# Decode-state stores of a streaming encoder step: seven stores on the ScalarE queue become four on the SyncE queue, gathered in contiguous tiles

## The chip, the cores and the metric

The kernel runs on one core of one Trainium2 chip, as a single program. The metric is device time in microseconds. The engines are called PE (TensorE, matmul), PEld (its weight loads), DVE (VectorE), ACT (ScalarE), POOL (GpSimd) and SP (SyncE). SP computes nothing here: it issues DMAs. ACT issues DMAs too, between its own instructions. "ACTq" and "SPq" in a row are those issuing queues. L1127 is line 1127 of the kernel before.

## What is computed

One layer for two groups of requests: a prompt of 4096 rows, and a decode group of 8 streams of 16 rows. A normalised, modulated input is projected to nine parts; three branches (pooling, short convolution, spatial gating) are gated, projected back and added to the input. The pooling and convolution branches keep a history, and the new history is an output:

```python
def pool_mix(p, hist, pos0, w_pool, pool_scale):
    full = jnp.concatenate([hist, p], axis=1)
    ...
    return out, full[:, -POOL_HIST:]      # last 15 rows of 256 channels

def conv_mix(q, hist, w_conv):
    full = jnp.concatenate([hist, q], axis=1)
    out = sum(w_conv[k] * full[:, k:k + L] for k in range(CONV_K))
    return out, full[:, -CONV_HIST:]      # last 2 rows of 384 channels

def layer(...):
    ...
    y_pool, new_pool = pool_mix(p, pool_hist, pos0, w_pool, pool_scale)
    y_conv, new_conv = conv_mix(gc * hx, conv_hist, w_conv)
    vn = layernorm(v, v_norm_g, v_norm_b)
    ...
    return x + gate[:, None] * y, new_pool, new_conv, vn
```

For the decode group the outputs are `nps` (new pooling history, 8 streams of 15 rows), `ncs` (new convolution history, 8 streams of 2 rows) and `nvs` (the rows of vn); `npp` and `ncp` are the prompt's histories.

## The kernel before

The prompt is worked in eight blocks of 512 rows, the decode group as a ninth of 128 (8 streams of 16). Channels lie on the 128 partitions, rows along the free dimension. Float32 values are split in a high and a low half-precision part, and each product is three half-precision matmuls. Each block goes through an input stage (`in_block`, or `in_dec` for the decode group) and an output stage (`out_block`); the output stage of a block is issued after the input stage of the next one. So `in_dec` stands between the output stage of prompt block 6 and that of prompt block 7 (the `ox`, `oy`, `oz` matmuls of L1246), and the decode group's own output stage (L1287) ends the program.

**Weights** come from DRAM through a ring of 18 slots of 256 KB (tile `ws`, L224, on SP's queue), up to 16 slots ahead of use, in the order in which PE uses them. In `in_dec` these are eight pieces `w_v_parts`, four `w_pool_in_parts` and forty `w_in_parts`.

**in_dec** (L1097) multiplies v (`z_v`, L819), then the two pooling tiles (`pool_in`, `z_p`), then three convolution tiles (`conv(j)`), the two pooling outputs (`pool_out`) and three gating tiles. Each `plain()` is a product of 60 small matmuls on four weight slots (24 on two slots with `only1`), all of them `z` in the rows. `conv(j)` calls it twice. Its steps:

- ACT copies the first product out of PSUM (`gc`, L1122); POOL copies two history rows per stream in front (`q`, L1127; `q` has two buffers, so the third waits till the first is free); DVE writes the 16 new rows behind (L1128); ACT stores the last two rows of each stream to `ncs` (L1129).
- ACT and DVE apply the three taps (`c`, L748 and L750), DVE and ACT empty the second pair of products (L1132, and `sz`, L1134), and the result goes to `ya` (L739), whose size ACT measures (L743).

`pool_in(i)` writes 16 rows per stream behind 15 of history in `pe_s` (L1151) and the prompt's tail to `ph` (L1152), and ACT stores 15 rows per stream to `nps` (L1153). POOL makes the window sums (L774), DVE the differences `d` (L777). `pes` was filled by two loads from `stp` (L1451), one per channel half. `gmlp_v` normalises v; in the decode case DVE also makes `vn` (L855, L856), which ACT stores to `nvs` (L857). At the end of `in_dec` ACT stores `ph` to `npp` (L1181).

**The order on each queue** is made by the tile scheduler: it simulates the program, then writes one fixed instruction list for each engine, so the place of an instruction in the source isn't its place in the list. Each engine runs its list in order; a DMA stands in the list of the engine that issues it, and its waits hold up all that follows there. The framework gives every DMA of SP and ACT one of eight completion counters, `DMAHW0` to `DMAHW7`, in turn, whichever queue it is on; a DMA is issued only when the last one on its counter has landed.

In the stretch in question ACT also stores four result tiles of prompt block 6 (`out_y`, L1231, 512 KB each), which DVE finishes at L1230.

Of the kernel before, what the change touches and what calls it, by code (L numbers as in the profile page):

```python
# [10 lines left out]
F32 = mybir.dt.float32  # L11
# [7 lines left out]
P = 128  # L19
# [4 lines left out]
NB = 8  # L24
ND = 16
# [6 lines left out]
HIST = 15  # L32
# [44 lines left out]
def trunk_kernel(ctx, tc, x, xs, xT, xsT, cT, wada, bada, badag, ng, win, winpT, wout, wpool, pscale, wconv,  # L77
# [746 lines left out]
    def gmlp_v(b, vh, ts, given):  # L824

        c = inv_of["v", 0]
        if "cv2" not in state:
            state["cv2"] = con.tile([P, 1], F32, name="cv2")
            nc.vector.tensor_tensor(state["cv2"], c, c, ALU.mult)
        tt = len(ts)  # L830
        st = sm.tile([P, 2, 6], F32, tag="bst", name="bst", bufs=2)
        mv = sm.tile([P, 2, 2], F32, tag="bmv", name="bmv", bufs=2)
        pss = []
        for j, t in enumerate(ts):
            ps = given[j]
            nc.vector.bn_stats(st[:, j, :], ps)
            nc.vector.bn_aggr(mv[:, j, :], st[:, j, :])
            pss.append(ps)
        var = sm.tile([P, tt], F32, tag="var", name="var", bufs=2)
        nc.vector.tensor_scalar(var, mv[:, :tt, 1], state["cv2"], EPS, ALU.mult, ALU.add)  # L840
        r = rsqrt(var, tt)
        a = sm.tile([P, tt], F32, tag="va", name="va", bufs=2)
        nb = sm.tile([P, tt], F32, tag="vb", name="vb", bufs=2)
        nc.vector.tensor_scalar(a, r, c, 2.0 ** 10, ALU.mult, ALU.mult)
        nc.vector.scalar_tensor_tensor(nb, mv[:, :tt, 0], -1.0, a, ALU.mult, ALU.mult)
        for j, t in enumerate(ts):
            v = tp.tile([P, 384], F32, tag="v32", name="v32", bufs=2)
            nc.vector.tensor_scalar(v, pss[j], a[:, j:j + 1], nb[:, j:j + 1], ALU.mult, ALU.add)
            v3 = seg(v, 64)
            nc.scalar.copy(vh[:, 0, :, t, :], v3)  # L850
            nc.vector.tensor_tensor(vh[:, 1, :, t, :], v3, vh[:, 0, :, t, :], ALU.subtract)
            if b.dec:
                gb = state["gbl"]
                vn = tp.tile([P, 384], F32, tag="v32", name="vn", bufs=2)
                nc.vector.scalar_tensor_tensor(vn, v, 2.0 ** -10, gb[:, 0, :], ALU.mult, ALU.mult)  # L855
                nc.vector.tensor_tensor(vn, vn, gb[:, 1, :], ALU.add)  # L856
                nc.scalar.dma_start(nvs, vn)  # L857

    def gmlp_mix(b, i, vh):

# [236 lines left out]
    def in_dec(b, H):  # L1097
# [20 lines left out]
        def conv(j):  # L1118
            gcp, hxp = plain(2 * j)
            f = lambda g: inv_of[g, j]  # L1120
            gc = temp("gc", n)
            nc.scalar.activation(gc, gcp, AF.Identity, scale=f("gc"))  # L1122
            q = tp.tile([P, BT + 2], F32, tag="q", name="q", bufs=2)
            q = q[:, :NB * (ND + 2)].rearrange("p (s f) -> p s f", f=ND + 2)
            c = temp("c", n)
            at = lambda i: q[:, :, i:i + ND]
            nc.gpsimd.tensor_copy(q[:, :, 0:2], G["stc"][:, j])  # L1127
            nc.vector.scalar_tensor_tensor(at(2), seg(hxp), f("hx"), seg(gc), ALU.mult, ALU.mult)  # L1128
            nc.scalar.dma_start(ncs[:, j], q[:, :, ND:])  # L1129
            conv_taps(j, q, seg(c), at)  # L1130
            gbp, zcp = plain(2 * j + 1)
            nc.vector.scalar_tensor_tensor(c, gbp, f("gb"), c, ALU.mult, ALU.mult)  # L1132
            s = temp("sz", n)
            nc.scalar.activation(s, zcp, AF.Silu, scale=f("zc"))  # L1134
            finish(b, 2 + j, c, s, ya, ym)

        def pool_in(i):
            inv = state["pinv"]
            ps = psum("z_p")[:, :n + ND]
            for kh in range(2):  # L1140
                product(ps, as_parts(stream.get()), h(kh, n + ND), kh == 0, kh == 1)
            stream.ahead(4)
            wi = inv[:, i:i + 1]

            def ext(name):
                t = tp.tile([P, BT + 16], F32, tag="pw", name=name, bufs=4)
                return t[:, :NB * 32].rearrange("p (s f) -> p s f", f=32)

            cut = lambda t, a, z=None: t[:, :, a:z]
            pe, d = state["pes"][:, i], temp("d", n)  # L1150
            nc.scalar.activation(pe[:, :, 16:], seg(ps[:, :n]), AF.Identity, scale=wi)  # L1151
            nc.scalar.activation(G["ph"][:, i, :], ps[:, n + 1:], AF.Identity, scale=wi)  # L1152
            nc.scalar.dma_start(nps[:, i], pe[:, :, 17:])  # L1153
            for _ in windows(i, pe, seg(d), cut, ext):
                pass
            return d
# [17 lines left out]
        for i in range(3):  # L1174
# [3 lines left out]
            s = temp("sz", n)  # L1178
            nc.scalar.activation(s, zp, AF.Silu, scale=inv_of["zg", i])
            finish(b, 5 + i, m, s, ya, ym)  # L1180
        nc.scalar.dma_start(npp, G["ph"])  # L1181
        return ya, ym


# [247 lines left out]
    for b in blocks:  # L1432
        if b.dec:
            ya, ym = in_dec(b, H)
        elif b.i > 0:
            ya, ym = in_block(b, H)
        stream.ahead()
        if not b.dec:
            nb = blocks[b.i + 1]
            if nb.dec:  # L1440
                H = hprep_dec(nb, load_stats(nb))
                state["G"]["mixer"] = mixer(state["G"], True)
                mixer_bias(state["G"])
                last = hop.tile([P, 2, D], F32, tag="t", name="xg_s")
                nc.sync.dma_start(last[:, 0, :], xs)
                nc.sync.dma_start(last[:, 1, :], gsd)
                state["last"] = last
                pes = hop.tile([P, 2, NB, 2 * ND], F32, tag="S2", name="pe_s")
                gbl = hop.tile([P, 2, 384], F32, tag="S1", name="gb_ln")
                for i in range(2):  # L1450
                    nc.sync.dma_start(pes[:, i, :, 1:16], stp[:, i])  # L1451
                    nc.sync.dma_start(gbl[:, i, :], (lngr, lnbr)[i].broadcast_to([P, 384]))
                state["pes"], state["gbl"] = pes, gbl
            else:
                H = h_tiles()
                h_plain(H, state["t"])
                h_sums(H, state["t"])
        got = {}

        def mid(b=b, ya=ya, ym=ym, got=got):  # L1460
            got["iy"], got["sy"] = scale_y(ym)
            if b.dec:
                got["yh"] = split_y(b, ya, got["sy"])

        def done(b=b, ya=ya, got=got):
            if not b.dec:
                got["yh"] = split_y_fast(ya, got["sy"]) if b.i >= OUT_FAST else split_y(b, ya, got["sy"])
            return b, got["yh"], got["iy"]

        if b.i == 0:  # L1470
            state["first"] = lambda mid=mid, done=done: (mid(), state.update(prev=done()))
        else:
            out_block(*state["prev"], mid)
            state["prev"] = done()
# [92 lines left out]
```

## Time and profile before

| | us |
|---|---|
| time, median of 3 runs | 1446.16 |
| lowest and highest of the 3 | 1443.79, 1448.75 |
| the profiled execution's own time | 1448.44 |
| its span, first to last instruction | 1446.40 |
| PE busy | 1375.5 (95% of the span) |
| DVE busy | 998.8 (69%) |
| ACT busy | 639.6 (44%) |
| POOL busy | 112.4 (8%) |
| PE granted clock, mean | 0.987 |

How to read it: the span is that of one profiled execution; its own time has 2.04 us around the span. A row of a timeline gives start, duration, engine, line, operation, output tile and inputs, count, and in brackets how long the engine had stood idle before and what it then waited for. "issue" is waiting for which the profile shows no cause. In a row on DMAs, "us to landing" runs from the issue to the arrival of the last byte. PEclk is the granted clock as a share of full speed; the DMA share is the mean busy share of the core's 16 DMA engines (sums of packet times, so it can pass 1).

### The profile page before, as it was taken

Reading aid. Unit: us, or ns where it says so; the run is one execution under the profiler, and the core shown is the slowest. Engines: PE = TensorE matmul, PEld = TensorE weight load, DVE = VectorE, ACT = ScalarE, POOL = GpSimd, SP = SyncE. Lnnn points to the kernel's source line nnn. Section 1 sums busy time; section 2 is a strip of 40 time slices with the busy share of each in tenths; the row PEclk is TensorE's granted clock in tenths of the full one; section 3 lists DMA queues with packets and bytes.
Section 4 is the critical chain, followed back from the end, with each engine's and each line's share of the span. In section 5 each row is a group of like instructions: output and inputs, shape, how many; then the busy total and the mean of one; then the engine's idle time right before and its main releaser. Section 6 shows DMA issues by size and latency. Waiting matters only on the chain.

```text
span 1446.4 us, 27018 instructions
## 1 busy us (share of the span) xinstructions
PE 1375.5 (95%) x10228; PEld 963.8 (67%) x10228; DVE 998.8 (69%) x2109; ACT 639.6 (44%) x1232; POOL 112.4 (8%) x150
## 2 busy tenths in 40 slices
PE   5898999999999999999999999999999999999697
PEld 2443454684688747885688758884788568866563
DVE  4764798787896678777775668567955777356535
ACT  3765756653356344443453435544443344223111
POOL 0000200020020102000020002000100002001000
PEclk9999999999999999999999999999999999999889
DMA  9687955994769659787797769888776768778995
GB/s 361 225 301 254 344 162 208 371 368 137 261 205 346 217 164 343 252 296 257 246 323 257 203 221 353 280 281 314 274 261 199 210 214 274 201 227 240 224 286 167
DMA packets 188292, 373.30 MB, mean 258 GB/s; under 512 B 28801, under 2 KB 40833, under 8 KB 188161
## 3 DMA queue, kind: packets, MB, share of 16 engines
q1 hardware_dynamic: 176480, 351.92, 73.6%
q10 hardware_dynamic: 11680, 19.65, 3.8%
q8 instruction: 80, 1.31, 0.4%
q14 instruction: 52, 0.42, 0.1%
HBM read 311.10 MB, written 60.39 MB: 257 GB/s over the span
## 4 chain that ended last, share of the span: by engine, by line
PE 55%; DVE 14%; DMA 9%; ACT 3%; issue 2%; POOL 0%; SPq 0%; ACTq 0%; DVEq 0%
PE zx L676 17%; PE ox L1246 9%; PE zy L676 8%; PE ps_o L1313 5%; PE zz L676 4%; PE oy L1246 4%; PE z_v L819 2%; PE oz L1246 2%; DVE xr L1230 2%; DVE yh L161 1%; DMA xt<-in_x 1%; DMA ws<-w_in_parts 1%; DMA w_out_sums<-wt 1%; DVE d L777 1%; PE z L676 1%
## 5 line engine op out<-in xcount | busy, mean ns | idle before, releaser
L676 PEld LDWEIGHTS <-ws 128*128 128x128 f16 x6360 | 600.2, 99 | 120.9 <-issue 23.8
L676 PE MATMUL zx<-A,ws 128*128 128x256 f16 x1572 | 182.6, 273 | 2.3 <-DVE nzg L708 1.0
L676 PE MATMUL zy<-S,ws 128*128 128x256 f16 x1572 | 184.4, 273 | 0.1
L676 PE MATMUL zx<-S,ws 128*128 128x256 f16 x1440 | 169.6, 273 | 10.2 <-ACT nu L700 8.1
L1246 PEld LDWEIGHTS <-yh 128*128 128x128 f16 x1008 | 98.1, 98 | 116.1
L676 PEld LDWEIGHTS <-wp 128*128 128x128 f16 x1056 | 103.4, 99 | 74.6 <-issue 5.8
L1246 PE MATMUL ox<-ws,yh 128*128 128x512 f16 x576 | 128.6, 379 | 0.0
L676 PE MATMUL zq<-A,wp 128*128 128x512 f16 x528 | 115.6, 379 | 0.0
L819 PE MATMUL z_v<-ws,A 128*128 128x384 f16 x696 | 115.1, 326 | 0.0
L676 PE MATMUL zz<-A,ws 128*128 128x256 f16 x852 | 101.3, 273 | 0.0
L819 PEld LDWEIGHTS <-A 128*128 128x128 f16 x696 | 68.1, 98 | 46.3 <-DVE A L330 0.2
L160 ACT ACTIVATE yh<-ya,sy 128x1024 f16<-128x1024 f32 (+1 forms) x58 | 57.6, 1025 | 65.0 <-PE ox L1246 17.0
L1313 PE MATMUL ps_o<-ws,yh 128*128 128x512 f16 x384 | 83.6, 379 | 0.0
L161 DVE SCALAR_TENSOR_TENSOR yh<-ya,sy,yh 128x1024 f16<-128x1024 f32 (+1 forms) x58 | 64.6, 1137 | 7.7 <-ACT yh L160 7.6
L1225 ACT ACTIVATE junk<-xr 128x1024 bf16<-128x1024 f32 x32 | 33.4, 1045 | 80.5 <-DVE xr L1254 50.0
L1313 PEld LDWEIGHTS <-yh 128*128 128x128 f16 x384 | 37.4, 98 | 44.2
L1254 DVE SCALAR_TENSOR_TENSOR xr<-ox,io,xr 128x512 f32<-128x512 f32 x48 | 34.0, 745 | 46.8 <-PE ox L1246 43.7
L1246 PE MATMUL oy<-ws,yh 128*128 128x512 f16 x288 | 64.3, 379 | 0.0
L676 PE MATMUL zq<-A,ws 128*128 128x512 f16 x288 | 62.5, 379 | 0.0
L760 POOL COPY qh<-q 128x2 f32<-128x2 f32 x24 | 7.6, 318 | 588.8 <-DVE q L759 588.8
L750 DVE SCALAR_TENSOR_TENSOR c<-q,wconv_sb,c 128x512 f32<-128x512 f32 (+1 forms) x54 | 38.0, 704 | 17.4 <-ACT c L748 16.6
L676 PE MATMUL z<-A,ws 128*128 128x128 f16 x588 | 39.8, 235 | 9.1 <-ACT sz L1134 5.8
(289 smaller groups left out, 1911.2 us busy)
## 6 DMA issues: line engine op xcount, KB each, us to landing
ws<-w_in_parts SPq DMA_DIRECT2D x517, 256.0 KB, 4.5
ws<-w_out_parts SPq DMA_DIRECT2D x104, 256.0 KB, 4.8
ws<-w_out_sums SPq DMA_DIRECT2D x96, 256.0 KB, 4.2
w_in_parts<-wp SPq DMA_DIRECT2D x83, 256.0 KB, 4.8
t<-in_xT SPq DMA_DIRECT2D x32, 512.0 KB, 6.9
xr<-in_x SPq DMA_DIRECT2D x32, 512.0 KB, 6.4
out_y<-xr ACTq DMA_DIRECT2D x32, 512.0 KB, 5.8
xt<-in_x SPq DMA_DIRECT2D x28, 512.0 KB, 6.6
```

Of the source, the lines that this page charges most:

```text
L160: nc.scalar.activation(dst_hi, src, AF.Identity, scale=s)
L161: nc.vector.scalar_tensor_tensor(dst_lo, src, s, dst_hi, ALU.mult, ALU.subtract)
L676: nc.tensor.matmul(ps, w[:, a, k, :], h[:, c, k, :], start=first and i == 0, stop=last and i == 3 * KH - 1, skip_group_check=True)
L750: nc.vector.scalar_tensor_tensor(c, at(i), wc[:, j, i:i + 1], c, ALU.mult, ALU.add)
L760: nc.gpsimd.tensor_copy(G["qh"][:, j, :], q[:, n:n + 2])
L777: nc.vector.scalar_tensor_tensor(dv[rows], cut(sums[e], 16)[rows], state["G"]["cinv"][rows, i:i + 1], cut(pe, 16)[rows], ALU.mult, ALU.sub ...
L819: nc.tensor.matmul(pss[t], H[1 + k // KH][:, a, k % KH, t * P:(t + 1) * P], w[:, e, :], start=k == 0 and i == 0, stop=k == KT - 1 and i == 2)
L1225: nc.scalar.activation(junk.bitcast(BF16), xts[t], AF.Square, accum_out=ss[:, j:j + 1])
L1230: nc.vector.scalar_tensor_tensor(xts[t], xts[t], r[:, j:j + 1], state["O"]["fg"], ALU.mult, ALU.mult)
L1246: nc.tensor.matmul(pss[bank][t], op[p][:, a, k, t * P:(t + 1) * P], w[:, c, 0, :], start=first and k == 0 and i == 0, stop=k == KH - 1 and ...
L1254: nc.vector.scalar_tensor_tensor(xt, pss[bank][t], io[:, hf:hf + 1], xt, ALU.mult, ALU.add)
L1313: nc.tensor.matmul(pss[t], yh[:, a, k, t * P:(t + 1) * P], w[:, c, 0, :], start=k == 0 and i == 0, stop=k == KT - 1 and i == 2)
```

## The change

The last 15 pooling rows of each stream are no longer stored from `pe` by two DMAs; POOL copies them into one tile (`stp_s`), and the last two convolution rows into the tile that held the old ones (`stc_sb`). Each tile is stored by one DMA, written at the end of `in_dec`, on SP's queue. `npp` and `nvs` move to SP's queue too. The pooling history is loaded into `stp_s` by one DMA, and POOL copies it into `pes`.

```diff
--- before.py
+++ after.py
@@ -854,7 +854,7 @@
                 vn = tp.tile([P, 384], F32, tag="v32", name="vn", bufs=2)
                 nc.vector.scalar_tensor_tensor(vn, v, 2.0 ** -10, gb[:, 0, :], ALU.mult, ALU.mult)
                 nc.vector.tensor_tensor(vn, vn, gb[:, 1, :], ALU.add)
-                nc.scalar.dma_start(nvs, vn)
+                nc.sync.dma_start(nvs, vn)
 
     def gmlp_mix(b, i, vh):
 
@@ -1126,7 +1126,7 @@
             at = lambda i: q[:, :, i:i + ND]
             nc.gpsimd.tensor_copy(q[:, :, 0:2], G["stc"][:, j])
             nc.vector.scalar_tensor_tensor(at(2), seg(hxp), f("hx"), seg(gc), ALU.mult, ALU.mult)
-            nc.scalar.dma_start(ncs[:, j], q[:, :, ND:])
+            nc.gpsimd.tensor_copy(G["stc"][:, j], q[:, :, ND:])
             conv_taps(j, q, seg(c), at)
             gbp, zcp = plain(2 * j + 1)
             nc.vector.scalar_tensor_tensor(c, gbp, f("gb"), c, ALU.mult, ALU.mult)
@@ -1150,7 +1150,7 @@
             pe, d = state["pes"][:, i], temp("d", n)
             nc.scalar.activation(pe[:, :, 16:], seg(ps[:, :n]), AF.Identity, scale=wi)
             nc.scalar.activation(G["ph"][:, i, :], ps[:, n + 1:], AF.Identity, scale=wi)
-            nc.scalar.dma_start(nps[:, i], pe[:, :, 17:])
+            nc.gpsimd.tensor_copy(state["stp"][:, i], pe[:, :, 17:])
             for _ in windows(i, pe, seg(d), cut, ext):
                 pass
             return d
@@ -1178,7 +1178,9 @@
             s = temp("sz", n)
             nc.scalar.activation(s, zp, AF.Silu, scale=inv_of["zg", i])
             finish(b, 5 + i, m, s, ya, ym)
-        nc.scalar.dma_start(npp, G["ph"])
+        nc.sync.dma_start(npp, G["ph"])
+        nc.sync.dma_start(nps, state["stp"])
+        nc.sync.dma_start(ncs, G["stc"])
         return ya, ym
 
 
@@ -1447,8 +1449,11 @@
                 state["last"] = last
                 pes = hop.tile([P, 2, NB, 2 * ND], F32, tag="S2", name="pe_s")
                 gbl = hop.tile([P, 2, 384], F32, tag="S1", name="gb_ln")
+                states = hop.tile([P, 2, NB, HIST], F32, tag="A2s", name="stp_s")
+                state["stp"] = states
+                nc.sync.dma_start(states, stp)
                 for i in range(2):
-                    nc.sync.dma_start(pes[:, i, :, 1:16], stp[:, i])
+                    nc.gpsimd.tensor_copy(pes[:, i, :, 1:16], states[:, i])
                     nc.sync.dma_start(gbl[:, i, :], (lngr, lnbr)[i].broadcast_to([P, 384]))
                 state["pes"], state["gbl"] = pes, gbl
             else:
```

What the scheduler makes of it is seen in the lists. PE's list is the same but for one instruction pair (`ps_sum`, L152, of the decode group), which moves from among the first `oy` matmuls of block 7 to behind its second row of `ox`; DVE's changes order in a few places round it.

ACT, in `in_dec`, from the second `out_nps` to the taps of conv 1. Before:

```order
L1153 DMA out_nps<-pe_s 128x8x15 [waits DMAHW3_49,Activation_49]
L160 ACTIVATE yh<-ya,sy 128x1024 [waits DVE_49]
L1181 DMA out_npp<-ph 128x30 [waits DMAHW5_49,Activation_49]
L1122 ACTIVATE gc<-z_16289,w_i 128x128 [waits PE_49]
L160 ACTIVATE yh<-ya,sy 128x1024 [waits DVE_49]
L1129 DMA out_ncs<-q 128x8x2 [waits DMAHW4_49,DVE_49]
L748 ACTIVATE c<-q,wconv_sb 128x128
L1134 ACTIVATE sz<-z_16382,w_i 128x128 [waits PE_49]
L1122 ACTIVATE gc<-z_16444,w_i 128x128 [waits PE_49]
L743 ACTIVATE sz,ym<-ya 128x128 [waits DVE_49]
L1129 DMA out_ncs<-q 128x8x2 [waits DMAHW1_49,DVE_49]
L748 ACTIVATE c<-q,wconv_sb 128x128
```

The same place in the change:

```order
L160 ACTIVATE yh<-ya,sy 128x1024 [waits DVE_49]
L1122 ACTIVATE gc<-z_16291,w_i 128x128 [waits PE_49]
L160 ACTIVATE yh<-ya,sy 128x1024 [waits DVE_49]
L748 ACTIVATE c<-q,wconv_sb 128x128 [waits DVE_49]
L1134 ACTIVATE sz<-z_16384,w_i 128x128 [waits PE_49]
L1122 ACTIVATE gc<-z_16446,w_i 128x128 [waits PE_49]
L743 ACTIVATE sz,ym<-ya 128x128 [waits DVE_49]
L748 ACTIVATE c<-q,wconv_sb 128x128 [waits DVE_49]
L1233 DMA out_y<-xr 128x1024 [waits DMAHW0_49,DVE_49]
L1134 ACTIVATE sz<-z_16539,w_i 128x128 [waits PE_49]
```

The stores and their waits for a counter have left ACT's list; `out_y` (now L1233) stays, on other counters.

SP, where the weights of the decode part are loaded, in the change (before, the same list without the rows of `out_npp`, `out_nps` and `out_ncs`):

```order
L1181 DMA out_npp<-ph 128x30 [waits DMAHW0_49,Activation_49]
L224 DMA ws<-w_in_parts 128x1024 [waits DMAHW1_49,PE_49]
L224 DMA ws<-w_in_parts 128x1024 [waits DMAHW2_49,PE_49]
L1182 DMA out_nps<-stp_s 128x240 [waits DMAHW3_49,Pool_49]
L224 DMA ws<-w_in_parts 128x1024 [waits DMAHW4_49,PE_49]
...
L1272 DMA xr<-in_x 128x1024 [waits DMAHW2_49,DVE_49]
L1183 DMA out_ncs<-stc_sb 128x48 [waits DMAHW3_49,Pool_49]
L224 DMA ws<-w_in_parts 128x1024 [waits DMAHW4_49,PE_49]
```

The stores stand between weight loads: `out_nps` ahead of the 21st of the forty `w_in_parts`, `out_ncs` behind the first `xr` load, with two `w_in_parts` and the output weights behind it; `out_nvs` comes five weight loads and two `xr` later. The one load of `stp` stands in SP's list between the first loads of `w_ada`, at the program's start.

POOL, in `in_dec`, in the change:

```order
L1153 COPY stp_s<-pe_s 128x120 [waits Activation_49]
L774 TENSOR_TENSOR pw<-pe_s 128x8x30
L774 TENSOR_TENSOR pw<-pw 128x8x28 [waits Pool_49]
L1153 COPY stp_s<-pe_s 128x120 [waits Activation_49]
L774 TENSOR_TENSOR pw<-pe_s 128x8x30
L774 TENSOR_TENSOR pw<-pw 128x8x28 [waits Pool_49]
L774 TENSOR_TENSOR pw<-pw 128x8x24 [waits DVE_49,Pool_49]
L774 TENSOR_TENSOR pw<-pw 128x8x16 [waits Pool_49]
L1129 COPY stc_sb<-q 128x16 [waits DVE_49]
L1127 COPY q<-stc_sb 128x8x2 [waits DVE_49,Activation_49,Pool_49]
L1129 COPY stc_sb<-q 128x16 [waits DVE_49]
L1129 COPY stc_sb<-q 128x16 [waits DVE_49,Pool_49]
```

The five rows that write `stp_s` and `stc_sb` are new; the third copy into `q` (L1127) no longer waits for a DMA counter. Two more copies, from `stp_s` into `pe_s`, stand earlier, in the input stage of prompt block 7.

## Rows read from the trace of the kernel before

**Rows 1.** Busy time by stretch; columns are in its first line, clock and DMA last.

```profile
core 0: us, PE busy (x) PEld busy (x) DVE busy (x) ACT busy (x) POOL busy (x), PEclk, DMA share, GB/s
1335.00:1340.00 5.00, 5.00 (x94) 5.00 (x91) 4.94 (x11) 2.10 (x3) 3.07 (x4) 1.00 1.26 197
...
1355.00:1360.00 5.00, 0.00 (x0) 0.00 (x0) 0.50 (x3) 0.37 (x1) 0.20 (x1) 0.65 1.26 187
...
1375.00:1380.00 5.00, 1.81 (x18) 1.81 (x18) 1.31 (x4) 1.72 (x8) 0.00 (x0) 0.50 0.97 179
...
1385.00:1390.00 5.00, 5.00 (x93) 5.00 (x91) 1.51 (x5) 1.11 (x4) 0.00 (x0) 1.00 1.04 394
```

**Rows 2.** Timeline of PE, decode part: start us, us, line op tile xcount [idle before].

```profile
1332.16 14.23 PE L676 MATMUL z<-A,ws 128*128 128x128 f16 x252
...
1353.35 0.84 PE L676 MATMUL z<-A,ws 128*128 128x128 f16 x12 [1.16 <-DMA ws<-w_in_parts]
...
1354.03 0.44 PE L1160 MATMUL ps_pl<-d,wpool_sb 128*128 128x128 f32 x2
...
1360.04 2.72 PE L676 MATMUL z<-A,ws 128*128 128x128 f16 x24 [5.57 <-ACT sz L1134]
...
1370.33 0.40 PE L869 MATMUL ps_mix<-wmix_s,vh 128*128 128x128 f16 x2 [3.44 <-DVE c L750]
...
1378.19 0.48 PE L869 MATMUL ps_mix<-wmix_s,vh 128*128 128x128 f16 x3 [3.21 <-DVE mix L871]
...
1390.13 5.34 PE L1246 MATMUL ox<-ws,yh 128*128 128x512 f16 x24
```

**Rows 3.** Chain that ended last, decode part: start us, us, what.

```profile
1335.37 10.09 DMA ws<-w_in_parts
...
1345.54 13.61 DMA out_ncs<-q
...
1384.82 0.17 PE ps_mix L869 x3
```

**Rows 4.** Timeline of ACT, decode part.

```profile
1345.96 0.40 ACT L748 ACTIVATE c<-q,wconv_sb 128x128 f32<-128x128 f32 x1 [5.39 <-DMA ws<-w_in_parts]
...
1359.62 0.37 ACT L1134 ACTIVATE sz<-z,w_i 128x128 f32<-128x128 f32 x1 [5.41 <-DMA out_ncs<-q]
...
1364.97 0.37 ACT L1122 ACTIVATE gc<-z,w_i 128x128 f32<-128x128 f32 x1 [4.99 <-DMA ws<-w_in_parts]
...
1369.47 0.40 ACT L748 ACTIVATE c<-q,wconv_sb 128x128 f32<-128x128 f32 x1 [3.84 <-DMA out_y<-xr]
...
1376.84 0.31 ACT L743 ACTIVATE sz<-ya 128x128 f32<-128x128 f32 x1 [6.30 <-DMA xr<-in_x]
```

**Rows 5.** Timeline of POOL, then of DVE, decode part.

```profile
1335.68 2.62 POOL L774 TENSOR_TENSOR pw<-pw 128x224 f32<-128x224 f32 x3
...
1340.96 0.34 DVE L1128 SCALAR_TENSOR_TENSOR q<-z,w_i,gc 128x128 f32<-128x128 f32 x1
...
1348.62 4.87 DVE L1230 SCALAR_TENSOR_TENSOR xr<-xr,rs_r,fgain 128x1024 f32<-128x1024 f32 x4
```

**Rows 6.** DMA queues, 1334 to 1346 us; q10 is ACT's.

```profile
DMA packets 3253, 2.02 MB, mean 168 GB/s; under 512 B 2344, under 2 KB 2344, under 8 KB 3251
...
q10 hardware_dynamic: 2224, 0.14, 24.5%
```

**Rows 7.** DMA issues, 1260 to 1447 us: count, KB each, median us to landing.

```profile
ws<-w_in_parts SPq DMA_DIRECT2D x43, 256.0 KB, 5.9
...
out_nps<-pe_s ACTq DMA_DIRECT2D x2, 60.0 KB, 11.5
out_ncs<-q ACTq DMA_DIRECT2D x3, 8.0 KB, 9.7
```

**Rows 8.** Instructions on tile stc_sb: ns min/median/max, first and last start.

```profile
L1127 POOL COPY q<-stc_sb x3: 198/638/1027, 1270.5 to 1359.3; 128x16 f32<-128x16 f32 x3
```

**Rows 9.** Busy time by stretch, 1325 to 1350 us (columns as in rows 1).

```profile
1325.00:1350.00 25.00, 24.73 (x386) 22.89 (x385) 21.10 (x43) 11.39 (x20) 5.71 (x6) 1.00 1.01 233
```

## The prediction

> **What bounds the kernel now.** TensorE (PE) is busy for most of the span, so only a stretch in which it stands still can pay. The stretches come first: PE does nothing at all from 1355 to 1360 us and 1.81 us of the five from 1375, at a granted clock of 0.65 and 0.50 (the lower of its two levels, 1.2 of 2.4 GHz); ten microseconds later it is full again [rows 1]. This is the decode part (in_dec). Then PE's own timeline there [rows 2]: 252 z matmuls run without a gap in 14.23 us from 1332.16, 56.5 ns each; later come 24 that waited 5.57 us for ACT's sz (L1134), a ps_mix that waited 3.44 us and one that waited 3.21; the out block of the last prompt block begins at 1390.13. From 1353.35 to 1390.13 are 36.8 us. The work in them at full clock: nine plain() products of 60 z matmuls and two of 24 are 588; the 12 at 1353.35 are the last of the 360 of the convolutions, so 240 are left, at 56.5 ns 13.6 us; two ps_pl pairs, at 0.44 us 0.9; nine ps_mix groups at 0.17 [rows 3], 1.5. That makes 16.0 us: **20.8 us of the stretch are waiting or slow clock**, and 1.16 us of idle stand just before it.
>
> Who makes PE wait: ACT. It sat idle 5.39, 5.41, 4.99, 3.84 and 6.30 us ahead of five small ACTIVATEs, each behind a store that ACT issues [rows 4]. What a store waits for is told by the program's order: each DMA of SP and ACT takes one of eight counters in turn (DMAHW0 to 7 in the rows of the change) and waits until the last DMA on that counter has landed. The chain shows what that costs [rows 3]: the first out_ncs is issued at 1345.54, 10.09 us after the weight load on its counter; out_ncs itself, 8 KB, takes 13.61 us, and out_y, next on that counter, waits for it. The value that out_ncs stores had been written by DVE by 1341.3 [rows 5].
>
> Why the DMAs are so slow: from 1334 to 1346 there are 2344 packets under 512 B among 3253, and 168 GB/s [rows 6], while in 1385 to 1390 engines no busier move 394 GB/s [rows 1]. An out_nps of 60 KB lands in 11.5 us and an out_ncs in 9.7, a weight load of 256 KB in 5.9 [rows 7]. The small packets are these stores: pe[:, :, 17:] is 8 runs of 60 B in each of 128 partitions, q[:, :, ND:] 8 runs of 8 B, so 1024 pieces per store and 5120 for the five.
>
> **The change part by part.**
>
> 1. *Five stores of 1024 pieces become two of 128 rows.* 5120 small packets go, 256 come. The 12 us from 1334 moved 2.02 MB; at 394 GB/s that takes 5.1 us, so 2344 small packets cost about 6.9 us of all engines, 2.9 ns each, and 5120 about 15 us. This does not add to the sum: it is why the waits of rows 4 are as long as they are.
>
> Here trace and page part. The Trainium skill, "DMA: Bandwidth & Descriptors", section "Why small descriptors are slow (HBM only)", puts a fixed overhead of about 3 cycles on each packet, and the page gives the fabric 850 MHz; an estimate from that page is 4 to 5 cycles for a piece of 8 or 60 B, some 1.7 us over 16 engines for all 5120. By it the change would free about a tenth of the 15 us; the row decides, and a chip on which small packets are cheap is rival B.
>
> 2. *Seven DMA issues leave ACT.* What counts is not the issue but that ACT is in order. Walked through: ACT's c of conv 0 starts when q is there, 1341.4 in place of 1345.96 [rows 4, 5]. DVE waits for it, but has a wide split to finish first; I take 3.2 us earlier, so that the four L1230, which now end at 1353.5 [rows 5], end near 1350.3. The four out_y stay on ACT. They now wait for L1230 and for weight loads: the 32nd slot of the decode part, in a ring of 18, is free when PE has used its 14th, at 15 matmuls a slot 1344.0, and lands 5.9 us later. So the last out_y goes out near 1350.5 and gc of conv 2 runs at 1350.9, not 1364.97. c of conv 2 follows at 1352.6, not 1369.47, for no store stands ahead of it; v32, vh and the first ps_mix come near 1356, not 1370.33. PE has done its six conv products by about 1352.5 and the two pool products by 1356. The nine ps_mix and three pairs of z products behind need 11.7 us at full clock, and out_nvs no longer holds the sz behind it (6.30 us). The out block starts near 1368 to 1369.5, 20.5 to 22 us earlier than 1390.13.
>
> Another section of that page, "Issuing engines are not separate DMA queues", says that issuing from several engines saves only the time the issue takes. By it this step would be worth some 3 us of ACT, from the page's logic and seven issues. The trace differs: rows 4 show 3.8 to 6.3 us of waiting ahead of issues, which the rule does not count.
>
> 3. *Five copies on POOL between compute steps.* Two for stp, three for stc. The nearest rows are its copies of 128x16, 0.20 to 1.03 us [rows 8]; I take the median, 0.64. The stp copies stand ahead of window sums, whose last now ends at 1338.3, while DVE reaches the d in front of q at about 1340.7 [rows 5]: 0.4 to 2.1 us fit in 2.4 us of slack, cost nothing. If that cover goes, the copies delay q one for one. The stc copies have nothing behind them but one another. The two copies into pe_s need a tile that block 7's S2 leaves long before the decode part: nothing.
>
> 4. *Four stores on SP,* each ahead of loads. Behind out_nps stands the 21st weight slot of the decode part; PE needs it after 300 z matmuls, near 1349, and a load takes 5.9 us: SP may stand at out_nps until 1343. SP gets there after 1335.37, when it issues the load ahead of that place [rows 3]; the copy is done by 1337.8 at the latest (the sums behind it began at 1335.68 [rows 5], plus 2.1). So SP is held for 2.4 us at most, hidden by the ring. out_ncs stands behind an xr load that waits for the first out_y to land (1347 and 5.9 or more), and q of conv 2 is there by 1352.5: nothing. vn is written near 1355.5, and SP comes to out_nvs later: nothing.
>
> 5. *One load of stp in place of two of 1024 pieces.* It moves to the start, between the w_ada loads: 120 KB at 394 GB/s, 0.3 us taken as lost. The two old loads kept no engine waiting; dropping them could give back up to 1 us of DMA time, which I leave out.
>
> 6. *PE's ps_sum (L152) moves behind a row of out matmuls;* the split it feeds is needed only by the last product of the program, 36 us after 1390: nothing.
>
> **Sum:** 20.8 + 1.16 are to be had; kept are an estimated 1 us of waits round the first ps_mix groups and 0.3 us at the start: 20.6 us. The profiled execution took 1448.44 (span 1446.40 and 2.04 around it), 2.28 over the median; from the median of 1446.16 this leaves **1425.6 us**. Its own bounds: the whole 22 us and 2.4 for the spread of runs, 1421; two thirds of the gain, 1432.
>
> **Rivals.**
>
> *A. The wait moves to out_y.* The four stores of 512 KB stay on ACT with their counters, and gc of conv 2 behind them. From 1335 to 1369 some 24 weight slots, four out_y and four xr have to pass, 10.5 MB or 309 GB/s, four fifths of 394. For it: the engines are full now. Against it: much of that fullness is small packets. If only the 233 GB/s of 1325 to 1350 [rows 9] came through, the same bytes would take 45 us: the out block at 1380, about **1436**.
>
> *B. Small packets are cheap,* and the DMAs are slow for another reason, such as stores mixed with loads. Then counters still free late; ACT is spared only the waits at the third out_ncs and at out_nvs, 3.84 and 6.30 us, of which I let half reach PE: **1441**. Against it: 8 KB in 13.61 us.
>
> *C. Nothing moves:* the stores "at the end" are in fact issued in the middle of the stream, as the rows of the change show, and the waits turn up on SP: **1446**.
>
> *D. Slower: SP held at out_nps* by POOL, with the weight stream behind it. For it: DVE is busy 4.94 of 5 us there [rows 1], and POOL's sums wait for it. Against it: copies of 1.03 us at most. It decides from 7.6 us of hold (1335.4 to 1343); each further microsecond costs one, and some 33 us of hold would eat the gain and give **1451**.
>
> **How the numbers follow.** A measurement of this kernel tells about 0.3%, 4.3 us, from no change. My forecast (1421 to 1432) has 0.72, A 0.14, B 0.06, C 0.05, D 0.03. Faster: forecast, A and most of B, 0.91; same: C and the rest of B, 0.06; slower: D, 0.03. The range for 8 in 10 takes the forecast's span and A's nearer half: 1421 to 1436.
>
> **What would show it.** Right: no crowd of small packets from 1334 to 1376 and 300 GB/s or more; out_nps and out_ncs landing in under 7 us; ACT's waits ahead of c (L748) and sz (L1134) under 1.5 us; PE's gaps of 5.57 and 3.21 us gone and its clock at 1.00; the out block some 21 us earlier, and little changed before 1330. Wrong: an ACT wait of 4 us or more at out_y (A), GB/s as low as now without small packets (B), SP standing at out_nps (D).

## The result and the profile after

The changed kernel takes **1425.71 us** (median of 6 runs, 1421.87 to 1430.53), the kernel before 1446.68 in 6 runs taken beside it: ratio 0.9857, 95% interval 0.9838 to 0.9875. That is 21.0 us faster by the medians, against 20.6 predicted. The profiled execution is the shortest of its six (1421.87, span 1420.1), that of before was one of its longer ones (1448.44), so the two traces differ by more than the medians, 26.3 us of span. PE is busy 1367.7 us in place of 1375.5: 7.8 us of the 26.3 are instructions of PE that got shorter, 7.0 of them in the decode part, where the granted clock averaged 0.79 and is now 1.00; the other 18.5 are idle time that is gone.

Busy time by stretch, changed kernel (columns as in [rows 1]):

```profile
1325.00:1350.00 25.00, 25.00 (x427) 24.54 (x426) 24.66 (x56) 10.90 (x25) 8.36 (x12) 1.00 1.02 365
1350.00:1375.00 25.00, 25.00 (x297) 18.74 (x295) 10.13 (x28) 4.43 (x18) 0.00 (x0) 1.00 1.02 377
...
1335.00:1340.00 5.00, 5.00 (x93) 5.00 (x91) 4.94 (x10) 2.17 (x4) 1.74 (x3) 1.00 1.01 361
1355.00:1360.00 5.00, 5.00 (x93) 5.00 (x91) 1.16 (x4) 1.14 (x4) 0.00 (x0) 1.00 1.02 346
```

PE is full in all 50 us, at a granted clock of 1.00; the five microseconds from 1355 in which it did nothing [rows 1] are full too. The engines of the DMAs are as busy as before (1.01 to 1.02) but move 365 GB/s from 1325 to 1350 where they moved 233 [rows 9].

Timeline of PE, decode part, changed kernel:

```profile
1329.13 20.26 PE L676 MATMUL z<-A,ws 128*128 128x128 f16 x360
1349.23 0.44 PE L1160 MATMUL ps_pl<-d,wpool_sb 128*128 128x128 f32 x2
1349.51 1.50 PE L676 MATMUL z<-A,ws 128*128 128x128 f16 x24
...
1352.47 0.33 PE L869 MATMUL ps_mix<-wmix_s,vh 128*128 128x128 f16 x3
...
1361.73 0.33 PE L869 MATMUL ps_mix<-wmix_s,vh 128*128 128x128 f16 x3
1361.90 1.78 PE L676 MATMUL z<-A,ws 128*128 128x128 f16 x29
1363.52 0.81 PE L1248 MATMUL ox<-ws,yh 128*128 128x512 f16 x3
```

No row has a bracket: the six longer waits of PE in the old stretch, 16.4 us together (the four of [rows 2], one of 2.11 and one of 0.87), are gone, and 24 z that took 2.72 us at the lower clock [rows 2] take 1.50. One measure serves for everything below, the **decode stretch**, from the first of these z to the first ox behind: 34.39 us here, 57.97 before (1332.16 to 1390.13). So 23.6 of the 26.3 us come from this stretch. 3.0 come from upstream of it, and I don't count them as the change's: that start lies anywhere from 1329.1 to 1335.5 in the twelve profiles of this study, with no order by what was edited. Behind the stretch the change needs 0.3 us more (56.3 and 56.6), which closes the sum.

ACT in the same part:

```profile
1338.39 0.40 ACT L748 ACTIVATE c<-q,wconv_sb 128x128 f32<-128x128 f32 x1 [0.91 <-DVE q L1128]
...
1343.67 0.34 ACTq L1233 DMA_DIRECT2D out_y<-xr  x1
1344.06 0.37 ACT L1134 ACTIVATE sz<-z,w_i 128x128 f32<-128x128 f32 x1 [1.37 <-PE z L676]
...
1344.87 3.14 ACTq L1233 DMA_DIRECT2D out_y<-xr  x3
1348.06 0.37 ACT L1122 ACTIVATE gc<-z,w_i 128x128 f32<-128x128 f32 x1 [3.63 <-PE z L676]
```

These answer to [rows 4], and the releaser has changed its name. There ACT waited for DMAs, 5.39 us at c and 5.41 at sz, and PE for ACT; now ACT waits for q and for PE's products. The four out_y are still on ACT, but no wait of ACT there ends on a DMA any more.

DMAs of the changed kernel, first 1334 to 1346 us (q1 is SP's queue: packets, MB, and the time of its packets as a share of 16 engines' span), then issue to landing in 1260 to 1421 us:

```profile
DMA packets 2437, 4.28 MB, mean 356 GB/s; under 512 B 320, under 2 KB 448, under 8 KB 2435
...
q1 hardware_dynamic: 2409, 4.15, 98.0%
...
ws<-w_in_parts SPq DMA_DIRECT2D x41, 256.0 KB, 4.9
...
out_nps<-stp_s SPq DMA_DIRECT2D x1, 120.0 KB, 4.6
out_ncs<-stc_sb SPq DMA_DIRECT2D x1, 24.0 KB, 5.8
```

320 small packets where there were 2344 [rows 6], and twice the bytes in the same 12 us. Each history now goes out in one DMA of whole rows, and the two land in 4.6 and 5.8 us where the stores in pieces took 11.5 and 9.7 [rows 7]. SP's queue in the kernel before, in the same 12 us:

```profile
q1 hardware_dynamic: 1027, 1.86, 86.5%
```

These two rows show where the engines' time went. ACT's 2224 packets, nearly all of them pieces, took 24.5% [rows 6], about 21 ns each on one engine; SP's packets, at nearly the same bytes each, took 162 ns each where they take 78 in the change. So, by these times, the larger part of the loss isn't the pieces' own time but SP's packets, nearly all of them weights, that took twice as long while the pieces were in the engines. Why they did, no run here shows.

### The profile page after: what moved, and what is told of

Read it like the earlier page. It is cut to its first block, busy times and chain, and to the rows that moved or that the text cites. A ratio compares the mean times of both kernels' runs of the same rounds, so it can differ in the third digit from the quotient of the medians.

```text
span 1420.1 us, 27016 instructions
## 1 busy us (share of the span) xinstructions
PE 1367.7 (96%) x10228; PEld 958.0 (67%) x10228; DVE 997.9 (70%) x2109; ACT 639.2 (45%) x1232; POOL 115.4 (8%) x157
## 4 chain that ended last, share of the span: by engine, by line
PE 62%; DVE 11%; DMA 7%; ACT 3%; issue 2%; POOL 0%; SPq 0%; DVEq 0%; ACTq 0%
PE zx L676 18%; PE zy L676 9%; PE ox L1248 9%; PE ps_o L1315 6%; PE zz L676 5%; PE z_v L819 5%; PE oy L1248 4%; PE z L676 2%; PE oz L1248 2%; DMA ws<-w_in_parts 2%; DVE xr L1232 1%; DMA xt<-in_x 1%; DVE d L777 1%; DMA st_wo<-in_wout 1%; PE ps_mix L878 1%
## 5 line engine op out<-in xcount | busy, mean ns | idle before, releaser
L763 ACT ACTIVATE nzc<-nzc 128x512 f32<-128x512 f32 x24 | 15.1, 628 | 74.5 <-DVE nzc L708 74.4
L774 POOL TENSOR_TENSOR pw<-pw 128x524 f32<-128x524 f32 (+5 forms) x36 | 47.9, 1330 | 8.4 <-DVE d L777 6.0
```

The costliest lines, as they stand in the source:

```text
L763: nc.scalar.activation(zc, zc, AF.Silu)
L774: nc.gpsimd.tensor_tensor(cut(s, lo), cut(sums[-1], lo), cut(sums[-1], lo - w, -w), ALU.add)
```

## The experiments

The change has two halves, the pieces and the queue, and the gain had to be split between them, then each half by store. All kernels ran beside the kernel before, whose median was 1446.39 in a first group of runs (pieces_only, queue_only, gathered_on_act, no_state_stores), 1443.95 in a second (nvs_on_act, all_but_nvs_on_act, nps_gathered, ncs_gathered) and 1442.37 in a third (nvs_alone_on_sp, pool_copies_x5), so across groups ratios are compared rather than times. A decode stretch is that of one profiled execution. "Small" is packets under 512 B, and MB what moved, both from 1325 to 1375 us of the profile; pieces are those of the five stores.

| kernel | pieces | out_nvs on | us (runs) | ratio, 95% interval | decode stretch | small, MB |
|---|---|---|---|---|---|---|
| before | 5120 | ACT | 1446.68 (6) | 1 | 57.97 | 5997, 12.14 |
| nps_gathered | 3072 | ACT | 1437.93 (12) | 0.9965, 0.9946 to 0.9984 | 46.12 | 4069, 15.08 |
| nvs_alone_on_sp | 5120 | SP | 1437.83 (12) | 0.9959, 0.9942 to 0.9977 | 45.75 | 5975, 13.17 |
| queue_only | 5120 | SP | 1437.44 (8) | 0.9941, 0.9916 to 0.9965 | 48.1 | 5978, 12.11 |
| nvs_on_act | none | ACT | 1433.17 (8) | 0.9932, 0.9904 to 0.9960 | 41.36 | 1261, 18.02 |
| ncs_gathered | 2048 | ACT | 1434.18 (7) | 0.9929, 0.9901 to 0.9958 | 43.16 | 3237, 16.46 |
| no_state_stores | none | ACT | 1432.60 (5) | 0.9907, 0.9876 to 0.9939 | 41.94 | 1110, 18.01 |
| pieces_only | none | ACT | 1430.39 (4) | 0.9901, 0.9869 to 0.9932 | 39.41 | 1784, 17.43 |
| gathered_on_act | none | ACT | 1430.94 (4) | 0.9901, 0.9868 to 0.9935 | 40.48 | 1244, 17.79 |
| pool_copies_x5 | none | SP | 1428.95 (6) | 0.9899, 0.9875 to 0.9922 | 35.52 | 1233, 17.65 |
| all_but_nvs_on_act | none | SP | 1425.95 (6) | 0.9875, 0.9843 to 0.9907 | 35.01 | 1260, 17.93 |
| the change | none | SP | 1425.71 (6) | 0.9857, 0.9838 to 0.9875 | 34.39 | 1294, 18.55 |

### The pieces alone: pieces_only

```diff
-            nc.scalar.dma_start(ncs[:, j], q[:, :, ND:])
+            nc.gpsimd.tensor_copy(G["stc"][:, j], q[:, :, ND:])
+            nc.scalar.dma_start(ncs[:, j], G["stc"][:, j])
...
-            nc.scalar.dma_start(nps[:, i], pe[:, :, 17:])
+            nc.gpsimd.tensor_copy(state["stp"][:, i], pe[:, :, 17:])
+            nc.scalar.dma_start(nps[:, i], state["stp"][:, i])
```

> Before, with the five stores of 1024 pieces made contiguous by a POOL copy in front of each (two of 128 rows of 480 B, three of 128 rows of 64 B); number, place and queue of the stores as before, all seven on ACT, old loads of the pooling history. Theory (the pieces are the cost, the engine that issues only feels it): the small packets between 1334 and 1346 us fall from 2344 to under 800, GB/s there rises over 300, out_ncs lands in under 7 us, ACT's waits ahead of c and sz shrink below 3 us each, decode stretch (first z matmul to the out block) from 58 to 35 to 42 us, time 1424 to 1432. Rival (the queue is the cost: stores in ACT's list hold ACT by their counters): ACT's waits stay 4 us and more, the stretch stays above 50 us, time 1440 to 1447.

Seven stores, still on ACT, still at the old places in the source; their pieces are gone. That alone is worth 0.99%, 14 us, and the stretch is 18.6 us shorter. In the 50 us from 1325 the kernel before, then this one, moves:

```profile
DMA packets 11178, 12.14 MB, mean 243 GB/s; under 512 B 5997, under 2 KB 5997, under 8 KB 11173
...
DMA packets 9179, 17.43 MB, mean 349 GB/s; under 512 B 1784, under 2 KB 1912, under 8 KB 9172
```

The difference, 5.29 MB at 349 GB/s, this kernel's rate there, takes 15.2 us: about what the prediction put on all 5120 pieces; spread over the 4213 small packets that are missing from the window it is some 3.6 ns each. What ACT still waits for is short, 2.83 us at the first out_y, 2.88 at the third out_ncs, 3.88 at out_nvs:

```profile
1348.59 0.37 ACT L1135 ACTIVATE sz<-z,w_i 128x128 f32<-128x128 f32 x1 [2.83 <-DMA out_ncs<-stc_sb]
...
1356.33 0.37 ACT L1135 ACTIVATE sz<-z,w_i 128x128 f32<-128x128 f32 x1 [2.88 <-DMA out_y<-xr]
...
1360.98 0.31 ACT L743 ACTIVATE sz<-ya 128x128 f32<-128x128 f32 x1 [3.88 <-DMA out_ncs<-stc_sb]
```

PE stands 1.48 us behind the second of these and 2.73 behind the third. One thing moved along with the pieces: in ACT's list each out_ncs now stands behind its c, where it stood in front of it. So this run by itself doesn't tell the pieces from that place; the rate, 391 GB/s from 1350 to 1375 in place of 252, speaks for the pieces, and nps_gathered below leaves the place as it was.

### The queue alone: queue_only

```diff
-                nc.scalar.dma_start(nvs, vn)
+                nc.sync.dma_start(nvs, vn)
...
-            nc.scalar.dma_start(ncs[:, j], q[:, :, ND:])
+            nc.sync.dma_start(ncs[:, j], q[:, :, ND:])
```

(and npp and the two nps in the same way)

> Before, with all seven stores issued by SP and not by ACT; five of them still in 1024 pieces, old loads. Theory (pieces): the crowd of small packets stays, 130 to 230 GB/s from 1334 to 1355; ACT loses its waits but SP, and with it the weights, now stands behind each slow store: at best half the gain, 1433 to 1447, and slower than before is possible if SP's list is held up by q or by counters. Rival (queue): ACT is free, the gain is there, 1424 to 1430.

0.59%. ACT in this kernel:

```profile
1355.01 0.34 ACTq L1231 DMA_DIRECT2D out_y<-xr  x1
1355.40 0.37 ACT L1134 ACTIVATE sz<-z,w_i 128x128 f32<-128x128 f32 x1 [11.76 <-DMA out_ncs<-q]
1356.62 6.17 ACTq L1231 DMA_DIRECT2D out_y<-xr  x3
1362.83 0.37 ACT L1122 ACTIVATE gc<-z,w_i 128x128 f32<-128x128 f32 x1 [7.07 <-DMA ws<-w_in_parts]
```

PE:

```profile
1355.82 2.72 PE L676 MATMUL z<-A,ws 128*128 128x128 f16 x24 [4.18 <-ACT sz L1134]
...
1363.25 2.72 PE L676 MATMUL z<-A,ws 128*128 128x128 f16 x24 [4.18 <-DMA ws<-w_in_parts]
```

This is rival A of the prediction, seen on its own: no state store is left on ACT, but it stands 11.76 us at the first out_y for an out_ncs that SP issued, because both queues share the eight counters. PE waits 4.18 us twice, first for the sz behind that out_y, then, by the profile, for a weight load, which SP's list now issues behind the same stores. The rate stays at 240 GB/s. Leaving the queue gives 0.59% of the 1.43%: an engine that still issues other DMAs keeps waiting as long as the slow transfers are there.

### Both halves, crossed: gathered_on_act

```diff
-                nc.sync.dma_start(nvs, vn)
+                nc.scalar.dma_start(nvs, vn)
...
-        nc.sync.dma_start(npp, G["ph"])
-        nc.sync.dma_start(nps, state["stp"])
-        nc.sync.dma_start(ncs, G["stc"])
+        nc.scalar.dma_start(npp, G["ph"])
+        nc.scalar.dma_start(nps, state["stp"])
+        nc.scalar.dma_start(ncs, G["stc"])
```

(the changed kernel with its four stores on ACT)

> The changed kernel with its four stores (npp, nps, ncs, nvs) issued by ACT and not by SP. Theory (pieces): nothing is slow any more, a counter frees in about 5 us, ACT stands at most 1 to 3 us at a store and PE's run ahead hides it: within 4 us of the changed kernel, 1424 to 1430. Rival (queue): ACT waits again at out_ncs and out_nvs, 3 to 6 us each, and PE with it: 1433 to 1440.

The same ratio as pieces_only: two stores or five make no difference once they are whole rows, nor does the one-piece load of stp. What the queue adds to gathered stores is the step from 0.9901 to 0.9857, some 6 us; the intervals still overlap a little (0.9869 to 0.9875).

### Without the five stores in pieces: no_state_stores

```diff
-            nc.scalar.dma_start(ncs[:, j], q[:, :, ND:])
...
-            nc.scalar.dma_start(nps[:, i], pe[:, :, 17:])
```

> Before without the five stores of nps and ncs: these two outputs are not written. It bounds what any way of storing them can give. Theory: no small packets, npp and nvs on ACT cost nothing once the engines are fast: 1423 to 1429, no faster than the changed kernel beyond its spread. Rival (npp and nvs on ACT matter by themselves): 1432 to 1440.

A miss, and the most useful run. This kernel leaves the two outputs unwritten, so it stores less than any other, and it moves more bytes a second than the change (392 GB/s against 377 from 1350 to 1375); it is slower than the change all the same. Its ACT:

```profile
1360.92 0.34 ACTq L857 DMA_DIRECT2D out_nvs<-vn  x1
1361.36 0.31 ACT L743 ACTIVATE sz<-ya 128x128 f32<-128x128 f32 x1 [6.41 <-DMA xr<-in_x]
```

The transfers are fast, and ACT stands 6.41 us, at out_nvs, whose counter an xr load of SP holds. That made out_nvs the suspect for the whole of the second half.

### out_nvs alone: nvs_on_act, all_but_nvs_on_act, nvs_alone_on_sp

Three kernels: the change with out_nvs put back on ACT; its complement, the other three on ACT and out_nvs on SP; and the kernel before with out_nvs alone moved. The edit of the first, and reversed of the last:

```diff
-                nc.sync.dma_start(nvs, vn)
+                nc.scalar.dma_start(nvs, vn)
```

> The changed kernel with one store put back: out_nvs on ACT's queue, the other three on SP's. Theory (the 5 us between gathered_on_act and the changed kernel are out_nvs alone: ACT stands 4 to 6 us at it for its counter, and the sz behind it holds up ps_mix): 1429 to 1432, ACT idle 3 us or more ahead of out_nvs, a gap of 3 us or more in PE at ps_mix. Rival (all four stores count, a little each; npp, nps and ncs as much as nvs): 1426 to 1428, no gap of PE over 1.5 us.

> The complement: npp, nps and ncs gathered and on ACT's queue, only out_nvs on SP's. Theory (out_nvs alone): 1424.5 to 1427.5, as the changed kernel, with no gap of PE over 1.5 us in the decode part. Rival (the other stores on ACT cost it): 1428 to 1431, and an ACT wait of 3 us or more ahead of a store other than out_nvs.

> The kernel before with out_nvs alone moved to SP's queue; the five stores in pieces and npp stay on ACT. Theory (the two parts add: ACT's standing at out_nvs costs about 5 us whatever stands ahead of it): 1438 to 1442 beside a before of 1444 to 1446, and no ACT wait over 2 us at out_nvs's old place. Rival (as long as the pieces are there, the other stores' waits end the stretch, and moving out_nvs alone gives nothing): 1443 to 1447.

The theory held in the first two: out_nvs on ACT costs the change what all four cost it or a little more (1433.17, 1.2 us over the range I gave; 0.9932 beside 0.9901, the intervals overlap), and with the other three on ACT and out_nvs on SP the ratio, 0.9875, is that of the change within the intervals. These two ran in the same group, and their medians lie 7.2 us apart. It held in the third too: among the pieces out_nvs is worth 0.41%, though there ACT's and PE's waits at the other stores stay (1437.83, 0.2 us under the range, beside a kernel before 1.6 us under what I had assumed). How one issue of 0.37 us does it can be followed through three engines of nvs_on_act. ACT:

```profile
1354.48 0.51 ACT L850 CAST vh<-v 128x384 f16<-128x384 f32 x1 [1.21 <-DVE v L848]
1360.62 0.37 ACTq L857 DMA_DIRECT2D out_nvs<-vn  x1
1361.09 0.31 ACT L743 ACTIVATE sz<-ya 128x128 f32<-128x128 f32 x1 [6.09 <-DMA out_ncs<-stc_sb]
...
1361.40 0.61 ACT L1163 ACTIVATE sz<-z,w_i 128x128 f32<-128x128 f32 x2
```

DVE, then PE:

```profile
1361.78 0.35 DVE L1164 SCALAR_TENSOR_TENSOR ya<-ps_pl,pscale_sb,sz 128x128 f32<-128x128 f32 x1 [5.34 <-ACT sz L1163]
1362.05 0.33 DVE L871 SCALAR_TENSOR_TENSOR mix<-ps_mix,wsg_s,wsb_s 64x128 f32<-64x128 f32 x1
```

```profile
1356.05 1.78 PE L676 MATMUL z<-A,ws 128*128 128x128 f16 x29
...
1362.43 0.48 PE L869 MATMUL ps_mix<-wmix_s,vh 128*128 128x128 f16 x3 [4.60 <-DVE mix L871]
```

vn was ready by 1356.2, yet out_nvs went out at 1360.62. In the program's lists out_ncs, on SP, and out_nvs, the eighth DMA behind it, have the same counter:

```
SP   L1183 DMA out_ncs<-stc_sb 128x48 [waits DMAHW3_49,Pool_49]
ACT  L857 DMA out_nvs<-vn 128x384 [waits DMAHW3_49,DVE_49]
```

SP issued out_ncs at 1355.40, and ACT could go on when it had landed. Behind out_nvs the pooling sz (L1163) was late, DVE stood 5.34 us at the ya that needs it, though the mix behind that ya was free to run, and PE stood 4.60 us at ps_mix for the mix, then ran its next rows at the lower clock (0.86 over 1350 to 1375). On SP out_nvs waits for the same counter, with only loads behind it, and PE shows no wait for them.

### The pieces, by store: nps_gathered, ncs_gathered

The kernel before with one of the two histories gathered by POOL and stored whole by ACT:

```diff
-            nc.scalar.dma_start(ncs[:, j], q[:, :, ND:])
+            nc.gpsimd.tensor_copy(G["stc"][:, j], q[:, :, ND:])
...
         nc.scalar.dma_start(npp, G["ph"])
+        nc.scalar.dma_start(ncs, G["stc"])
```

> Before with the pooling history alone gathered by POOL and stored by one DMA on ACT; the three out_ncs keep their 3072 pieces of 8 B, the loads are the old ones. Theory (cost goes by pieces, 5120 of them worth the 16 us of pieces_only): 2048 pieces go, 1439 to 1442. Rival (what costs is a store with small pieces in front of c and q, that is out_ncs): 1444 to 1447, with ACT's waits at c as long as before. Second rival (bytes: 120 of the 144 KB are nps): 1431 to 1435.

> Before with the convolution history alone gathered by POOL and stored by one DMA on ACT; the two out_nps keep their 2048 pieces of 60 B. Theory (by pieces): 3072 go, 1435 to 1439. Rival (the out_ncs in ACT's list are the cause): 1430 to 1433, as with all five gathered. Second rival (bytes): 1443 to 1446.

Gathering 120 KB of pooling history gives 0.35%, gathering 24 KB of convolution history 0.71%. So the theory of bytes (5 to 1) falls, and that of pieces (2 to 3) stands within the intervals (0.16 to 0.54% and 0.42 to 0.99%). nps_gathered came out 1 us under the range that I gave for it, and ncs_gathered 0.8, beside a kernel before that was itself 2.7 us faster in this group. The two gains and that of nvs_alone_on_sp add up to 1.47%; the change gives 1.43%, so by the times the three parts add. By the decode stretch they don't: the three single steps take 11.9, 14.8 and 12.2 us off it, 38.9 together, and the change 23.6. All of these are counted from one profile of the kernel before, a long execution, and the stretches start up to 6.4 us apart, so they can't decide it; that the parts are independent rests on the times, each with an interval of some 0.4 to 0.6%. That the out_ncs also stand in front of c in ACT's list, and so cost more a piece, is not excluded either: 0.71 is more than 1.5 times 0.35, and ncs_gathered takes three DMAs out of ACT's way and puts one back, nps_gathered only two for one.

### Does POOL's cover hold: pool_copies_x5

```diff
-            nc.gpsimd.tensor_copy(state["stp"][:, i], pe[:, :, 17:])
+            for _ in range(5):
+                nc.gpsimd.tensor_copy(state["stp"][:, i], pe[:, :, 17:])
```

> The changed kernel with each of the two POOL copies of the pooling history done five times over, so 8 copies more among the window sums, at 0.31 to 1.28 us each some 2.5 to 10 us of POOL work more. Theory (the copies are hidden: POOL has slack until DVE reaches the d ahead of q, and ACT's gc behind it still waits 3.63 us for PE): 1425 to 1428, PE without a gap. Rival (no cover: each microsecond of POOL delays d, q and then PE): 1429 to 1436, with a DVE wait on POOL of 3 us or more.

Between the two by the time: 1428.95, 3.2 us above the change, and its interval of the ratio only touches that of the change; by the ratios the difference is 0.42%, 6 us, as much as all the POOL work that was added. The trace stands nearer the theory, but it is that of the shortest of the six executions (1424.45). There POOL's copies take 7.05 us in place of 1.59, the last window sum ends 11.3 us behind the first z instead of 7.5, DVE waits 0.73 us for POOL, q of conv 0 is written 1.8 us later, PE waits 0.20 and 0.60 us, and the stretch is 1.1 us longer:

```profile
1339.28 0.34 DVE L777 SCALAR_TENSOR_TENSOR d<-pw,cinv_sb,pe_s 64x128 f32<-64x128 f32 x1 [0.73 <-POOL pw L774]
```

In that execution most of the 5.5 us of POOL work was hidden, not all; for the other five that isn't shown. SP and the DMAs show a second cover at work:

```profile
1331.87 6.73 SPq L224 DMA_DIRECT2D ws<-w_in_parts  x9
1341.64 0.34 SPq L1183 DMA_DIRECT2D out_nps<-stp_s  x1
```

```profile
1340.00:1345.00 5.00, 5.00 (x93) 5.00 (x91) 4.84 (x17) 1.71 (x6) 2.91 (x6) 1.00 0.59 191
```

SP stood 3.0 us at out_nps (1338.6 to 1341.64) for the copies, the DMA engines fell to 0.59 busy, and PE's 360 z ran through without a gap: the weights already in the ring of 18 slots carried it. The scheduler had also put seven more loads ahead of out_nps, so this is not rival D at its worst.

## Why the prediction was right, point by point

**The bound.** Right: a decode part held by ACT, which was held by its own stores. All of the gain that the traces can place is there, but for the 3.0 us upstream.

**Step 1, the pieces.** The size held: 15 us of engines and 2.9 ns a piece were forecast; pieces_only gives 15.2 us of engines, some 3.6 ns a piece, and 14 us of time. Worked out in the same way nps_gathered gives 5.1 ns (2.94 MB at 302 GB/s over 1928 small packets), so 2.9 was low rather than high. What the step had not seen is that the smaller part of it is the pieces' own time (24.5% of 12 us, 2.9 of the 6.9 us from 1334 to 1346, by the packets' times); the rest is that the weight packets beside them took longer. The rule of the Trainium skill, "DMA: Bandwidth & Descriptors", "Why small descriptors are slow (HBM only)", has the right direction; the estimate made from it, 1.7 us, was an eighth of what pieces_only got back. Rival B, that small packets are cheap, is out.

**Step 2, ACT.** Right in its course. Counted from the first z, c of conv 0 was forecast at 9.2 us and came at 9.3, the first ps_mix at 23.8 and came at 23.3; the out block was forecast at 35.8 to 37.3 and came at 34.4. Two small terms were mis-sized, both on the safe side. The work behind the conv products was counted as 15.3 us and took 14.13: the z behind a pair of ps_pl starts 0.28 us after it, not 0.44, and there are six groups of ps_mix, not nine; the two make 0.8 of the 1.2 us. And the 1 us that was kept for waits round the first ps_mix wasn't needed: no PE row has a wait. So the stretch gave 23.6 us between the two traces, where 20.6 were forecast, and the 21.0 of the medians is nearer than the steps were. That the total came within 0.4 us is in part luck: the waits were read off an execution 2.28 us above the median and taken off that median in full, and the steps then gave 3 us more than was forecast.

What the prediction had not seen is how the gain divides. It took step 2 for the gain and step 1 for its reason; the runs show that gathering gives two thirds of it with every store still on ACT, and that the queue then matters for one store, the last named in step 2 ("out_nvs no longer holds the sz behind it (6.30 us)"). The rule in the section "Issuing engines are not separate DMA queues" of that page of the Trainium skill is that another engine saves only the time of the issue; an estimate from it, with the issue of 0.37 us, is some 0.4 us for out_nvs. Moving it alone gave 0.41% among the pieces and, by the step from nvs_on_act to all_but_nvs_on_act, 0.57% without them: 6 to 8 us. The rule holds for bandwidth here (240 GB/s in queue_only, 233 before) and not for the engine that has to wait in order.

**Step 3, POOL.** Hidden, as said, though the second stp copy took 1.28 us, above the 1.03 that was given as the upper end:

```profile
1331.04 1.28 POOL L1153 COPY stp_s<-pe_s 128x120 f32<-128x120 f32 x1
...
1332.94 3.68 POOL L774 TENSOR_TENSOR pw<-pw 128x224 f32<-128x224 f32 x3
```

No wait of DVE in the decode part of the changed kernel ends on POOL. Five times the copies cost 1.1 us of the stretch in the one profile, where "one for one" beyond the slack is too strict, and 3 to 6 us by the medians, where it isn't refuted.

**Step 4, SP.** Right. In the changed kernel SP goes from out_nps to the next load in 0.6 us:

```profile
1332.34 0.34 SPq L1182 DMA_DIRECT2D out_nps<-stp_s  x1
1332.93 17.88 SPq L224 DMA_DIRECT2D ws<-w_in_parts  x18
```

**Steps 5 and 6** moved nothing that can be seen: gathered_on_act has the new load, pieces_only the old ones, and their ratios are the same; behind the stretch, where the ps_sum stands, the change needs 0.3 us more.

**Rivals.** A is real, but needs the pieces: it is queue_only. B and C are refuted by the DMA rows. D didn't occur; even in pool_copies_x5 SP was held 3.0 us, under the 7.6 from which D counted.

Most of the marks that were set came true: small packets, rate, landings, ACT's waits ahead of sz and c (1.37 and 0.91 us, under the 1.5), PE's gaps and its clock. The last two didn't, between these two traces: the out block comes 26.6 us earlier, not 21, and the decode part already starts 3.0 us earlier, where little was to change before 1330. Left open: why executions of one kernel differ by up to 12 us (before, 1437.6 to 1449.95 in the second group), and why the decode part starts up to 6.4 us apart in the profiles.

## What to carry to other kernels

Count the pieces of a store, not its bytes: 24 KB in 3072 pieces cost no less than 120 KB in 2048 (0.71% and 0.35%), and a copy of 0.2 to 1.3 us on an idle engine makes it one row per partition. Then look where each DMA stands in the list of an engine that also computes: with this framework's eight counters, what it costs is not its issue but the time until the eighth DMA before it, on whichever queue, has landed, and everything behind it in that list pays; move first the store that the critical engine's next consumer stands behind, here one of seven. And when a stretch is cured, the sign is not a smaller wait but another releaser: ACT now waits for PE.

## What the runs showed of the hardware

- Stores in runs of 8 and 60 B slowed the transfers that shared the engines with them: with the engines about fully busy in both, 50 us moved 12.14 MB with 5997 small packets in the kernel before and 17.79 MB with 1244 in gathered_on_act.
- Less traffic was no gain by itself. no_state_stores moves 0.14 MB less than the change has to, at 392 GB/s, and is 0.5% behind it, for one wait of 6.41 us.
- The slow clock came behind PE's waits and went away with them. Over 1350 to 1375 the granted clock was 0.70 in the kernel before, 0.73 in queue_only (4.18 us of idle twice), 0.86 in nvs_on_act (4.60), and 1.00 in pieces_only (2.73 at most) and in the change (none). ncs_gathered has 0.86 behind shorter waits (2.50, 1.43 and 1.75), so these runs give no length of idle from which it falls.
- While pieces were in the engines, the weight packets beside them took 162 ns each from 1334 to 1346, and 78 in the change.
